# Feed-forward gate and up in seven block products, with their result kept in float32

## The chip, the cores and the metric

One NeuronCore of a Trainium2 chip runs the whole program. The time is device microseconds (us) from the first to the last instruction of one execution. The kernel before takes 2728.88 us, the median of three runs (2725.41 to 2729.14).

## What is computed

A decoder trunk of two layers on 512 tokens of width 1024, in float32. Each layer is three residual steps, each followed by a layer norm:

```python
def swiglu(x, w_gate, w_up, w_down):
    return (jax.nn.silu(x @ w_gate) * (x @ w_up)) @ w_down

for l in range(DEPTH):                                   # DEPTH = 2
    x = layer_norm(ALPHA * x + 0.5 * swiglu(x, ffn1_gate[l], ffn1_up[l], ffn1_down[l]), ...)
    x = layer_norm(ALPHA * x + token_mixing(x, w_in[l], ...), ...)
    x = layer_norm(ALPHA * x + 0.5 * swiglu(x, ffn2_gate[l], ffn2_up[l], ffn2_down[l]), ...)
```

The hidden width of the feed-forward is 2816, 22 tiles of 128 features, so there are four feed-forward passes with 22 feature tiles each. `token_mixing` is a pair of attention branches (a selected/compressed/window one and a dilated one), a spatial gating unit, three merge gates and an output product.

## The kernel before, in words

**Precision.** TensorE multiplies in float32r. Every operand is held as two float32r parts, high and low, and a product is three matmuls: high by high, high by low, low by high (`mm3`, lines 367 to 369).

**Weights.** All weights are packed into blocks of [128, 1024] in the order of their use (`PLAN`). SyncE brings one after another into `raw` (3 buffers); `split_w` makes the high part on ScalarE (line 322) and the low part on VectorE, or on GpSimd in some stretches (line 325), into `wh` and `wl` (4 buffers). `pump` and `get_w` split ahead of use, two blocks in the feed-forward.

**Feed-forward.** x stands transposed as `xh`, `xl` in the first 64 blocks (of 128 columns) of the big tile `R`. For each of 22 feature tiles f, `ffn` multiplies the gate block and the up block with x: 8 row tiles by 3 matmuls of 512 columns, for each of the two. The first two feature tiles run in two halves of 256 columns, since they start while the last token tiles are still being transposed (`x_transposed`, lines 428 to 434). `post` then takes silu on ScalarE (line 575), the product on VectorE (line 578), and the high and low parts on VectorE (lines 387, 388); all 22 results stand in `R` until `tm_gemm` has used them. `tm_gemm` (the down product) runs two passes of 512 output columns; each weight block holds two row tiles and serves 24 matmuls. The last four blocks of a pass are held so that the token tiles finish one by one and residual and norm run beside the next tile.

**Mixers.** `weave` emits two generators in turn: attention steps as they become ripe, dense products in between. Their memory comes from the 168 other blocks of `R` (`ralloc`, first fit). Where a dense step finds no room it yields WAIT, and attention steps follow one another without dense products between them.

**Order.** The program is written out in the order of emission: each engine runs its own instructions in that order, and waits are semaphores on the data they need. What stands ahead of an instruction in its engine's list therefore delays it.

## Time and profile before

| | |
|---|---|
| median of three runs | 2728.88 us |
| profiled execution, first to last instruction | 2728.7 us |
| TensorE busy | 2654.7 us (97%), 13566 matmuls |
| VectorE busy | 1256.5 us (46%) |
| ScalarE busy | 871.5 us (32%) |
| GpSimd busy | 638.0 us (23%) |

The profiled execution lies within 0.2 us of the median, and its span is all of its time: nothing lies around it. A busy share is an average over the whole program. The program has stages of two kinds: feed-forward (about 26 to 372 us, 1000 to 1720 us and from 2360 us on) and mixers (372 to 1000 us and 1720 to 2360 us), and they are to be read apart.

### The profile page before, as it was taken

What the parts mean: (1) busy time and instruction counts of PE and PEld (TensorE: products, weight loads), DVE (VectorE), ACT (ScalarE), POOL (GpSimd) and SP (SyncE); (2) the same over time, 40 slices, a digit from 0 to 9 for tenths busy, and PEclk for the clock granted to TensorE, in tenths of its full rate; (3) what the DMA queues carried; (4) which work ended last, traced back from release to release, by engine and by line L of the source; (5) the groups of instructions that cost most, each with busy time, mean ns of one, the idle gap of its engine ahead of it and who ended that gap; (6) DMA issues with size and microseconds to landing.
All of it is one profiled execution on the core that took longest, in us unless ns stands there. A gap on an engine that the chain in (4) does not pass through costs nothing. (4 is left out here: it accounts for less than half of the span.)

```text
span 2728.7 us, 34447 instructions
## 1 busy us (share of the span) xinstructions
PE 2654.7 (97%) x13566; PEld 2256.6 (83%) x13566; DVE 1256.5 (46%) x2501; ACT 871.5 (32%) x1562; POOL 638.0 (23%) x563
## 2 busy tenths in 40 slices
PE   9999999999999999999999999999999999999998
PEld 8888889977778888888888888899777788888887
DVE  4333265667442463432443333656674424633334
ACT  3222134445642222221222222345455322222211
POOL 1000015554644510000010000246455454100000
PEclk9999999999999999999999999999999999999999
DMA  4223333111212333333233232222112134322332
GB/s 165 93 95 123 100 99 100 60 47 40 78 41 91 116 119 98 94 118 103 72 103 99 93 121 95 101 92 71 36 52 65 43 99 135 106 95 96 108 101 77
DMA packets 71170, 248.16 MB, mean 91 GB/s; under 512 B 8016, under 2 KB 10096, under 8 KB 71008
## 3 DMA queue, kind: packets, MB, share of 16 engines
q1 hardware_dynamic: 68832, 238.25, 26.8%
q0 software_dynamic: 2176, 7.71, 0.9%
q8 instruction: 106, 1.74, 0.3%
q14 instruction: 56, 0.46, 0.1%
HBM read 239.64 MB, written 6.29 MB: 90 GB/s over the span
## 5 line engine op out<-in xcount | busy, mean ns | idle before, releaser
L368 PE MATMUL P<-R,wh 128*128 128x512 f32 (+1 forms) x2144 | 810.3, 378 | 7.1 <-DVE R L434 7.1
L367 PE MATMUL P<-R,wh 128*128 128x512 f32 (+1 forms) x2144 | 811.0, 378 | 1.0 <-ACT R L431 1.0
L369 PE MATMUL P<-R,wl 128*128 128x512 f32 (+1 forms) x2144 | 809.0, 377 | 0.0
L322 ACT CAST wh<-raw 128x1024 fp32r<-128x1024 f32 (+3 forms) x445 | 449.3, 1015 | 861.5 <-PE P L368 371.6
L367 PE MATMUL P<-wh,R 128*128 128x512 f32 (+3 forms) x1600 | 582.8, 364 | 2.0 <-ACT R L431 2.0
L368 PE MATMUL P<-wl,R 128*128 128x512 f32 (+3 forms) x1600 | 572.7, 358 | 4.2 <-POOL wl L325 2.1
L369 PE MATMUL P<-wh,R 128*128 128x512 f32 (+3 forms) x1600 | 572.9, 358 | 2.3 <-DVE R L434 2.1
L325 DVE TENSOR_TENSOR wl<-raw,wh 128x1024 fp32r<-128x1024 f32 (+1 forms) x289 | 349.0, 1234 | 397.6 <-ACT wh L322 397.4
L325 POOL TENSOR_TENSOR wl<-raw,wh 128x1024 fp32r<-128x1024 f32 (+5 forms) x157 | 352.6, 2253 | 755.0 <-ACT wh L322 754.2
L368 PEld LDWEIGHTS P<-R,wh 128*128 128x128 f32 x2144 | 405.4, 189 | 82.7 <-DVE R L434 9.1
L367 PEld LDWEIGHTS P<-R,wh 128*128 128x128 f32 x2144 | 405.2, 189 | 75.8 <-ACT R L431 1.9
L369 PEld LDWEIGHTS P<-R,wl 128*128 128x128 f32 x2144 | 405.4, 189 | 74.1
L368 PEld LDWEIGHTS P<-wl,R 128*128 128x128 f32 x1600 | 304.1, 190 | 43.9 <-POOL wl L325 3.2
L369 PEld LDWEIGHTS P<-wh,R 128*128 128x128 f32 x1600 | 303.5, 190 | 44.1 <-DVE R L434 3.2
L367 PEld LDWEIGHTS P<-wh,R 128*128 128x128 f32 x1600 | 304.1, 190 | 40.4 <-ACT R L431 2.2
L578 DVE TENSOR_TENSOR Fa<-Fa,P 128x512 f32<-128x512 f32 x88 | 60.5, 688 | 541.6 <-PE P L369 538.8
L471 POOL DMA_DIRECT2D Fa<-in_ln_g x6 | 3.5, 584 | 772.5 <-DVE Fa L578 563.5
L575 ACT ACTIVATE Fa<-P 128x512 f32<-128x512 f32 x88 | 52.6, 598 | 366.6 <-PE P L369 366.6
L1428 POOL TENSOR_SCALAR Fa<-Fa,ac,ga 128x128 f32<-128x128 f32 (+3 forms) x128 | 78.1, 620 | 67.4 <-DVE ac L1424 56.2
L387 DVE CAST R<-Fa 128x512 fp32r<-128x512 f32 (+2 forms) x130 | 77.9, 599 | 33.8 <-POOL Fa L1158 26.7
L1456 DVE TENSOR_TENSOR R<-P,R 128x256 fp32r<-128x256 f32 (+2 forms) x96 | 54.5, 595 | 66.5 <-ACT R L1443 66.3
L644 ACT CAST R<-P 128x256 fp32r<-128x256 f32 (+3 forms) x176 | 49.9, 322 | 103.2 <-PE P L641 102.8
(155 smaller groups left out, 2165.4 us busy)
## 6 DMA issues: line engine op xcount, KB each, us to landing
raw<-in_wts SPq DMA_DIRECT2D x400, 512.0 KB, 3.5
raw<-in_wts SPq DMA_DIRECT2D x16, 480.0 KB, 3.4
x_sp<-Fa SPq DMA_DIRECT2D x8, 512.0 KB, 5.1
Fa<-x_sp SPq DMA_DIRECT2D x8, 512.0 KB, 4.9
Fa<-in_ln_g POOLq DMA_DIRECT2D x6, 512.0 KB, 4.2
Fa<-in_ln_b POOLq DMA_DIRECT2D x6, 512.0 KB, 4.4
raw<-in_wts SPq DMA_DIRECT2D x8, 320.0 KB, 2.8
Fa<-in_x SPq DMA_DIRECT2D x4, 512.0 KB, 6.3
```

The lines of the kernel that those rows point to most:

```text
L322: nc.scalar.copy(h, r)
L325: (nc.gpsimd if self.pool_lo or n == 1 else nc.vector).tensor_tensor(lo, r, hf, op=OP.subtract)
L367: mm(out, lh, rh, start=start, stop=False)
L368: mm(out, lh, rl, start=False, stop=False)
L369: mm(out, ll, rh, start=False, stop=stop)
L387: self.nc.vector.tensor_copy(hi, src)
L471: self.nc.gpsimd.dma_start(v[:, k * D:(k + 1) * D], row.to_broadcast([128, D]))
L575: nc.scalar.activation(s, self.P[bg], AF.Silu)
L578: nc.vector.tensor_tensor(h, s, self.P[bu], op=OP.mult)
L644: self.nc.scalar.copy(hi, src[ps, ks])
L1428: t.nc.gpsimd.tensor_scalar(e, e, rd[:, br:br + 1], t.ga[:, s["i"], c:c + 1], op0=OP.mult, op1=OP.mult)
L1456: self.t.nc.vector.tensor_tensor(lo, src, h, op=OP.subtract)
```

## The change

- The weight blocks of feature tiles 2 to 21 are packed as quarters: [gate rows 0-511 | up rows 0-511] and [up rows 512-1023 | gate rows 512-1023]. Seen as a 2 by 2 matrix of blocks (gate and up by the two halves of the inner width), times x as a 2 by 2 matrix (halves of the inner width by halves of the tokens), the eight block products become seven, on sums and differences of blocks. Each product is 4 row tiles by 3 matmuls of 256 columns.
- Four sums of weight blocks for each feature tile are made on GpSimd (`quad`); each of the seven left operands is then split by itself, 512 columns at a time. Eight half buffers are handed out as they come free, and the split runs up to eight products ahead (`LOOK`).
- Four sums of x blocks are made once for each pass (`x_sums`), from a float32 copy of x transposed.
- The results of the products are put together by copies on ScalarE and additions on VectorE as they leave PSUM; the second half of the last product is a GpSimd instruction.
- The product of silu(gate) and up stays in float32 (`H`); the down product makes its high and low parts as it goes, twice, once for each pass, in ten rotating buffers (`make`).
- `H` and the upper 80 of the 232 blocks of `R` are one memory, `H` in the feed-forward, `Rb` in the mixers. The mixers' allocator may not cross the seam at block 152, and the merged results stay below it.
- All 22 feature tiles were of the old kind; tiles 0 and 1 still are (`PLAIN`).

```diff
         for f in range(NF):
-            plan.append(("kcol", f"ffn{w}_gate", l, f * 128, 1024))
-            plan.append(("kcol", f"ffn{w}_up", l, f * 128, 1024))
+            for part in range(2):
+                if f < PLAIN:
+                    plan.append(("kcol", f"ffn{w}_" + ("gate", "up")[part], l, f * 128, 1024))
+                else:
+                    plan.append(("quad", f"ffn{w}", l, (f, part), 1024))
...
-RB, FB = 232, 44
+RB, R0, FB = 232, 152, 44
+HB = RB - R0
 EB, EA = 30, 24
 XB = NT * KT
-RAW, WB = 3, 4
+RAW, WB, LOOK = 3, 4, 8
...
-    def ralloc(self, n):
-        while (a := self.ra.alloc(n)) is None:
+    def ralloc(self, n, up=False):
+        while (a := (self.ra.alloc(n, R0, RB) if up else None) or self.ra.alloc(n)) is None:
...
-        (nc.gpsimd if self.pool_lo or n == 1 else nc.vector).tensor_tensor(lo, r, hf, op=OP.subtract)
+        (nc.gpsimd if kind == "full" and (self.pool_lo or j == 1) else nc.vector).tensor_tensor(lo, r, hf, op=OP.subtract)
+        if kind == "full":
+            self.raw_done[n] = True
+        else:
+            if q in self.sums:
+                self.fa.free(self.sums.pop(q)[0], 4)
+            self.raw_done[n] |= q == S1
+            self.raw_done[n + 1] |= q == A22
...
+    def quad(self, n, q):
+        a11, a21 = (self.raw[:, n % RAW, c:c + 512] for c in (0, 512))
+        a22, a12 = (self.raw[:, (n + 1) % RAW, c:c + 512] for c in (0, 512))
+        def add(k, x, y, op):
+            a, v = self.fbuf(4)
+            self.nc.gpsimd.tensor_tensor(v, x, y, op=op)
+            self.sums[k] = (a, v)
+            return v
+        if q == A11:
+            s1 = add(S1, a21, a22, OP.add)
+            add(S2, s1, a11, OP.subtract)
+        elif q == S1:
+            add(S3, a11, a21, OP.subtract)
+        elif q == A12:
+            add(S4, a12, self.sums[S2][1], OP.subtract)
+        return {A11: a11, A12: a12, A22: a22}[q] if q in (A11, A12, A22) else self.sums[q][1]
...
+    def dma_w(self, upto=len(PLAN)):
+        while self.n_dma < upto and (self.n_dma < RAW or self.raw_done[self.n_dma - RAW]):
...
-        while (self.n_split < len(PLAN) and self.n_split < self.n_got + look
-               and (self.n_split < WB or self.done_w[self.n_split - WB])):
+        while self.n_split < min(len(JOBS), self.n_got + look) and self.w_room(self.n_split) is not None:
...
+    def new_h(self):
+        assert not any(self.ra.used[R0:])
+        self.ra.used[R0:] = [True] * HB
+        self.H = self.pool.tile([128, HB * 128], F32, name="H", tag="hr", bufs=1)
+    def new_rb(self):
+        self.Rb = self.pool.tile([128, HB * 128], F32R, name="Rb", tag="hr", bufs=1)
...
+            if ffn:
+                nc.scalar.copy(xt[:, ks, ts], src)
...
+        if ffn and i >= 2:
+            self.x_sums(i - 2)
+    def x_sums(self, j):
+        nc = self.nc
+        xt = self.H[:, :4096].rearrange("p (a k t) -> p a k t", a=2, k=4)
+        b11, b21 = (xt[:, a, :, j * 128:(j + 1) * 128] for a in range(2))
+        b12, b22 = (xt[:, a, :, j * 128 + 256:(j + 1) * 128 + 256] for a in range(2))
+        t = [self.H[:, 4096 + (j * 4 + n) * 512:4096 + (j * 4 + n + 1) * 512].rearrange("p (k t) -> p k t", k=4)
+             for n in range(4)]
+        nc.vector.tensor_tensor(t[0], b12, b11, op=OP.subtract)
+        nc.gpsimd.tensor_tensor(t[2], b22, b12, op=OP.subtract)
+        nc.vector.tensor_tensor(t[1], b22, t[0], op=OP.subtract)
+        nc.gpsimd.tensor_tensor(t[3], b21, t[1], op=OP.subtract)
+        for n in range(4):
+            hi, hif, lo = (q[:, :, j * 128:(j + 1) * 128] for q in self.xt_views(n))
+            nc.scalar.copy(hi, t[n])
+            nc.vector.tensor_tensor(lo, t[n], hif, op=OP.subtract)
...
-            ha, h = self.fbuf(4)
-            nc.vector.tensor_tensor(h, s, self.P[bu], op=OP.mult)
+            nc.vector.tensor_tensor(H(f), s, self.P[bu], op=OP.mult)
             self.unbank(bu)
             self.fa.free(sa, 4)
-            r = 0 if f == NF - 1 else self.ra.alloc(8)
-            self.hilo_sb(self.rv(r, 4), self.rvf(r, 4), self.rv(r + 4, 4), h)
-            self.fa.free(ha, 4)
-            hh.append(r)
...
-        for f in range(2, NF):
-            b = [self.bank(), self.bank()]
-            for q in range(2):
-                w = self.get_w("kcol")
-                self.fm_proj(b[q], w)
-                self.put_w(w)
-            post(f, *b)
+        x_of = lambda c, k0: tuple(q[:, k0:k0 + 4, c:c + 256] for q in (self.xh, self.xl))
+        t_of = lambda n: self.xt_views(n)[::2]
+        right = {A11: x_of(0, 0), A12: x_of(0, 4), S4: x_of(256, 4), S1: t_of(0), S2: t_of(1), S3: t_of(2), A22: t_of(3)}
+        def product(st, q, b, more=False):
+            self.n_got = max(self.n_got, st["j"] + q + 1)
+            self.pump(0)
+            _, wh, wl = w = (st["j"] + q, *self.w_views(st["j"] + q)[::2])
+            rh, rl = right[q]
+            for k in range(4):
+                ks = slice(k * 128, k * 128 + 128)
+                self.mm3(self.P[b][:, :256], wh[:, ks], wl[:, ks], rh[:, k], rl[:, k],
+                         k == 0 and not more, k == 3, more)
+            self.put_w(w)
+            self.pump(LOOK)
+        def end(st):
+            f, b = st["f"], st["beta"]
+            product(st, A22, b, True)
+            nc.vector.tensor_tensor(H(f, slice(0, 256)), st["g"][:, :256], self.P[b][:, :256], op=OP.mult)
+            self.unbank(b)
+            nc.gpsimd.tensor_tensor(H(f, slice(256, 512)), st["g"][:, 256:], st["p"], op=OP.mult)
+            self.fa.free(st["ga"], 4)
+            self.fa.free(st["pa"], 2)
+        prev = None
+        for f in range(PLAIN, NF):
+            if f == HB // 4:
+                more.append(self.fbuf((NF - f) * 4))
+            st = {"f": f, "j": self.n_got}
+            st["ga"], st["g"] = self.fbuf(4)
+            st["pa"], st["p"] = self.fbuf(2)
+            g1, g2, p = st["g"][:, :256], st["g"][:, 256:], st["p"]
+            beta, gamma, alpha = st["beta"], _, _ = [self.bank() for _ in range(3)]
+            P = [self.P[b][:, :256] for b in (beta, gamma, alpha)]
+            product(st, A11, beta)
+            nc.scalar.copy(g1, P[0])
+            product(st, S1, gamma)
+            nc.scalar.copy(p, P[1])
+            product(st, A12, alpha)
+            nc.vector.tensor_tensor(g1, P[2], g1, op=OP.add)
+            self.unbank(alpha)
+            product(st, S2, beta, True)
+            nc.scalar.copy(g2, P[0])
+            if prev:
+                end(prev)
+            product(st, S4, gamma, True)
+            nc.vector.tensor_tensor(g2, P[1], g2, op=OP.add)
+            self.unbank(gamma)
+            nc.scalar.activation(st["g"], st["g"], AF.Silu)
+            product(st, S3, beta, True)
+            nc.vector.tensor_tensor(p, P[0], p, op=OP.add)
+            prev = st
             if l + j == 0 and f == 4:
                 self.load_consts()
+        end(prev)
+        self.ra.free(self.xt_at, 64)
+        base = self.ra.alloc(80)
+        made, used, hs = [0], [0], NT * 2
+        def make(n):
+            a = base + n % 10 * 8
+            v = H(n % NF)
+            self.nc.scalar.copy(self.rv(a, 4), v)
+            self.nc.vector.tensor_tensor(self.rv(a + 4, 4), v, self.rvf(a, 4), op=OP.subtract)
         def lhs(k):
-            r = hh[k]
-            return self.rv(r, 4), self.rv(r + 4, 4)
-        self.tm_gemm(lhs, NF, l, j, last)
-        for r in hh[:-1]:
-            self.ra.free(r, 8)
-    # ---- mixers ----
+            n = k if used[0] < NF else NF + k
+            while made[0] < min(max(n + 5, used[0] + 8), used[0] + 10, 2 * NF):
+                make(made[0])
+                made[0] += 1
+            assert made[0] > n >= used[0]
+            a = base + n % 10 * 8
+            return self.rv(a, 4), self.rv(a + 4, 4)
+        def done(k):
+            used[0] += 1
+        self.tm_gemm(lhs, NF, l, j, last, done)
+        self.ra.free(base, 80)
+        self.fa.free(more[0][0], (NF - HB // 4) * 4)
...
-            r = yield from self.ralloc(8)
+            while (r := self.ra.alloc(8, 64, R0)) is None:
+                yield WAIT
             self.mg.append(r)
```

**What the change moves in the lists of the engines.** Each list is in the order in which its engine runs it; "x2" is two of the same in a row.

**VectorE and GpSimd, one feature tile of gate and up.** Before, on VectorE (line 578 is the product with up, 387 and 388 its two parts, 325 the low parts of two weight blocks):

```order
L578 TENSOR_TENSOR Fa<-Fa,P_74 128x512
L387 CAST R<-Fa 128x512
L388 TENSOR_TENSOR R<-Fa,R 128x512
L325 TENSOR_TENSOR wl<-raw,wh 128x1024 x2
L578 TENSOR_TENSOR Fa<-Fa,P_76 128x512
```

GpSimd has no arithmetic in this stage before. Now VectorE has this for a feature tile (line 389 makes the low part of a left operand, from `raw` or from a sum in `Fa`; 784, 791 and 795 add what left PSUM; 763 is the first half of the last product):

```order
L389 TENSOR_TENSOR wl<-raw,wh 128x512
L389 TENSOR_TENSOR wl<-Fa,wh 128x512
L389 TENSOR_TENSOR wl<-raw,wh 128x512
L784 TENSOR_TENSOR Fa<-P_74,Fa 128x256
L389 TENSOR_TENSOR wl<-Fa,wh 128x512
L389 TENSOR_TENSOR wl<-raw,wh 128x512
L763 TENSOR_TENSOR H<-Fa,P_78 128x256
L389 TENSOR_TENSOR wl<-Fa,wh 128x512
L791 TENSOR_TENSOR Fa<-P_73,Fa 128x256
L389 TENSOR_TENSOR wl<-Fa,wh 128x512
L795 TENSOR_TENSOR Fa<-P_75,Fa 128x256
```

Seven splits of 512 columns stand where two of 1024 stood, and four instructions of 256 columns that read PSUM stand between them. GpSimd now has, for the same feature tile, the four sums (line 407) and half of the last product (line 765):

```order
L407 TENSOR_TENSOR Fa<-raw 128x512
L407 TENSOR_TENSOR Fa<-Fa,raw 128x512
L407 TENSOR_TENSOR Fa<-raw 128x512
L407 TENSOR_TENSOR Fa<-raw,Fa 128x512
L765 TENSOR_TENSOR H<-Fa 128x256
```

GpSimd's part of a feature tile is new, and each of its five instructions reads SBUF twice.

**VectorE and ScalarE, from gate and up to the down product of the first pass.** Before, on VectorE:

```order
L578 TENSOR_TENSOR Fa<-Fa,P_72 128x512
L387 CAST R<-Fa 128x512
L388 TENSOR_TENSOR R<-Fa,R 128x512
L325 TENSOR_TENSOR wl<-raw,wh 128x1024 x11
L477 SCALAR_TENSOR_TENSOR Fa<-P_77,Fa 128x512
```

The parts of the last feature tile were made by `post`; from there on only weight blocks were split (325), until the first residual (477). Now, on VectorE (809 makes the low part of a row tile of the down product):

```order
L791 TENSOR_TENSOR Fa<-P_76,Fa 128x256
L389 TENSOR_TENSOR wl<-raw,wh 128x1024
L795 TENSOR_TENSOR Fa<-P_78,Fa 128x256
L389 TENSOR_TENSOR wl<-raw,wh 128x1024
L763 TENSOR_TENSOR Fa<-Fa,P_78 128x256
L809 TENSOR_TENSOR R<-H,R 128x512 x10
L389 TENSOR_TENSOR wl<-raw,wh 128x1024
L809 TENSOR_TENSOR R<-H,R 128x512 x2
```

and on ScalarE (386 splits weights, 793 is silu, 808 makes the high part of a row tile):

```order
L787 COPY Fa<-P_78 128x256
L386 CAST wh<-raw 128x1024
L793 ACTIVATE Fa<-Fa 128x512
L386 CAST wh<-raw 128x1024 x2
L808 CAST R<-H 128x512 x10
L386 CAST wh<-raw 128x1024
```

The first ten row tiles of the down product are now split after the last product of gate and up, and behind the fourth split of a whole weight block.

**TensorE in the mixers, first layer, after the transposes that end the second projection of the dilated head 1.** Before, the projection of the next head followed (320 columns, lines 367 to 369):

```order
L641 MATMUL P_74<-ident,Fa 128x128 x2
L367 MATMUL P_75<-wh,R 128x320
L368 MATMUL P_75<-wl,R 128x320
L369 MATMUL P_75<-wh,R 128x320
L367 MATMUL P_75<-wh,R 128x320
L368 MATMUL P_75<-wl,R 128x320
```

Now an attention step follows there (lines 460 to 462 are `mm3`, 1504 and 1505 scores of the third group, 1547 transposes of weights):

```order
L845 MATMUL P_72<-ident,Fa 128x128 x2
L460 MATMUL P_77<-Rb 128x128
L461 MATMUL P_77<-Rb 128x128
L462 MATMUL P_77<-Rb 128x128
L460 MATMUL P_75<-Rb 128x128
L461 MATMUL P_75<-Rb 128x128
L462 MATMUL P_75<-Rb 128x128
L1504 MATMUL P_74<-R 128x128
L1505 MATMUL P_74<-R 128x128
L1547 MATMUL P_78<-ident,Fa 128x128 x2
L1547 MATMUL P_72<-ident,Fa 128x128 x4
L1547 MATMUL P_77<-ident,Fa 128x128 x4
```

The projection of that head comes later, because 18 blocks are free at this point but no run of 12 on one side of the seam; it is the same number of products in another order.

## Rows read from the trace of the kernel before

**Rows 1.** The page, parts 1 and 2: busy us, granted TensorE clock.

```profile
PE 2654.7 (97%) x13566; PEld 2256.6 (83%) x13566; DVE 1256.5 (46%) x2501; ACT 871.5 (32%) x1562; POOL 638.0 (23%) x563
...
PEclk9999999999999999999999999999999999999999
```

**Rows 2.** Busy time by stage: stretch, length, each engine, PEclk, DMA share, GB/s.

```profile
26.00:372.00 346.00, 346.00 (x1574) 288.38 (x1573) 131.25 (x166) 80.87 (x92) 4.34 (x6) 1.00 0.32 101
372.00:1000.00 628.00, 600.62 (x3391) 519.17 (x3390) 341.72 (x882) 263.01 (x582) 300.64 (x265) 0.98 0.25 79
...
1720.00:2360.00 640.00, 611.39 (x3447) 528.08 (x3446) 352.16 (x903) 267.00 (x588) 302.86 (x266) 0.98 0.24 79
```

**Rows 3.** Timeline of TensorE, gate and up at 512 columns: start, us, engine, line.

```profile
60.06 0.39 PE L369 MATMUL P<-R,wl 128*128 128x512 f32 x1
...
63.91 0.39 PE L368 MATMUL P<-R,wh 128*128 128x512 f32 x1
```

**Rows 4.** Timeline of VectorE, one feature tile of gate and up.

```profile
243.47 0.69 DVE L578 TENSOR_TENSOR Fa<-Fa,P 128x512 f32<-128x512 f32 x1 [6.73 <-PE P L369]
...
244.66 0.69 DVE L388 TENSOR_TENSOR R<-Fa,R 128x512 fp32r<-128x512 f32 x1
245.27 2.36 DVE L325 TENSOR_TENSOR wl<-raw,wh 128x1024 fp32r<-128x1024 f32 x2
254.35 0.69 DVE L578 TENSOR_TENSOR Fa<-Fa,P 128x512 f32<-128x512 f32 x1 [6.73 <-PE P L369]
```

**Rows 5.** Timeline of TensorE and its weight load, products of 256 columns.

```profile
13.10 0.28 PE L367 MATMUL P<-R,wh 128*128 128x256 f32 x1
...
16.10 0.28 PE L368 MATMUL P<-R,wh 128*128 128x256 f32 x1
16.10 0.19 PEld L369 LDWEIGHTS P<-R,wl 128*128 128x128 f32 x1
```

**Rows 6.** Groups by line and shape: busy us, mean ns | idle before.

```profile
L322 ACT CAST wh<-raw 128x1024 fp32r<-128x1024 f32 x399 | 417.3, 1049 | 848.3 <-PE P L368 371.6 <-PE P L369 348.1 <-issue 46.5
L575 ACT ACTIVATE Fa<-P 128x512 f32<-128x512 f32 x88 | 52.6, 598 | 366.6 <-PE P L369 366.6
...
L644 ACT CAST R<-P 128x256 fp32r<-128x256 f32 x64 | 22.2, 374 | 59.4 <-PE P L641 59.4
...
L648 DVE TENSOR_TENSOR R<-P,R 128x256 fp32r<-128x256 f32 x64 | 25.1, 416 | 14.4 <-ACT R L644 14.4
...
L1158 POOL TENSOR_TENSOR Fa<-Fa 128x512 f32<-128x512 f32 x32 | 41.3, 1289 | 28.5 <-DVE Fa L1154 28.2
```

**Rows 7.** Timelines of VectorE and GpSimd at the end of the first pass.

```profile
359.41 1.27 DVE L485 SCALAR_TENSOR_TENSOR Fa<-Fa,ac 128x1024 f32<-128x1024 f32 x1
...
372.36 6.29 POOL L325 TENSOR_TENSOR wl<-raw,wh 128x840 fp32r<-128x840 f32 x3 [147.40 <-ACT wh L322]
379.33 2.25 POOL L325 TENSOR_TENSOR wl<-raw,wh 128x960 fp32r<-128x960 f32 x1 [0.69 <-ACT wh L322]
...
375.35 2.47 DVE L434 TENSOR_TENSOR R<-P,R 128x512 fp32r<-128x512 f32 x4
...
379.50 3.17 DVE L485 SCALAR_TENSOR_TENSOR Fa<-Fa,ac 128x1024 f32<-128x1024 f32 x1
```

**Rows 8.** Timelines of TensorE and VectorE where the second pass starts.

```profile
998.71 0.39 PE L368 MATMUL P<-R,wh 128*128 128x256 f32 x1 [1.84 <-DVE R L434]
...
1006.56 1.28 DVE L434 TENSOR_TENSOR R<-P,R 128x512 fp32r<-128x512 f32 x2
1012.33 1.29 DVE L434 TENSOR_TENSOR R<-P,R 128x512 fp32r<-128x512 f32 x2 [4.49 <-ACT R L431]
```

**Rows 9.** Busy time in one stretch of a mixer without dense work.

```profile
540.00:560.00 20.00, 17.93 (x126) 16.25 (x125) 10.45 (x35) 8.60 (x22) 9.90 (x9) 0.91 0.17 54
```

**Rows 10.** The page, part 6: weight DMAs, KB each, us to landing.

```profile
raw<-in_wts SPq DMA_DIRECT2D x400, 512.0 KB, 3.5
```

More of the change, by code (lines that the diff above doesn't have):

```diff
@@ L33 @@
 GATES_AHEAD = 2
+PLAIN = 2
 def weight_plan():
@@ L94, with weight_jobs @@
 PLAN = weight_plan()
+def weight_jobs():
+    jobs = []
+    for n, p in enumerate(PLAN):
+        if p[0] != "quad":
+            jobs.append(("full", n, 0))
+        elif p[3][1] == 0:
+            jobs += [("quad", n, q) for q in range(7)]
+    return jobs
+JOBS = weight_jobs()
+A11, S1, A12, S2, A22, S4, S3 = range(7)
 def pack_weights(inp):
@@ L102, in pack_weights @@
             o[:].reshape(128, KT, 128)[...] = inp[name][l][:, a:a + 128].reshape(KT, 128, 128).transpose(1, 0, 2)
+        elif kind == "quad":
+            f, part = a
+            for h, nm in enumerate(("gate", "up") if part == 0 else ("up", "gate")):
+                src = inp[f"{name}_{nm}"][l][part * 512:part * 512 + 512, f * 128:f * 128 + 128]
+                o[:, h * 512:h * 512 + 512].reshape(128, 4, 128)[...] = src.reshape(4, 128, 128).transpose(1, 0, 2)
         elif kind == "rows":
@@ L192, in alloc @@
         for a in list(range(at, hi)) + list(range(lo, at)):
+            if self.seam and a < self.seam < a + n:
+                continue
             if a + n <= hi and not any(self.used[a:a + n]):
@@ L241, in __init__ @@
         self.n_dma = self.n_split = self.n_got = 0
-        self.done_w = [False] * len(PLAN)
+        self.raw_done = [False] * len(PLAN)
+        self.w_free = deque(range(2 * WB))
+        self.w_at = {}
+        self.sums = {}
         self.pool_lo = False
@@ L360, in put_w, with mm3 @@
     def put_w(self, w, look=0):
-        self.done_w[w[0]] = True
+        at, n = self.w_at[w[0]]
+        self.w_free.append(at)
+        if JOBS[w[0]][0] == "full":
+            self.w_free.append(at + 1)
         if look and not self.weaving:
             self.pump(look)
-    def mm3(self, out, lh, ll, rh, rl, start, stop):
+    def mm3(self, out, lh, ll, rh, rl, start, stop, more=False):
         mm = self.nc.tensor.matmul
-        mm(out, lh, rh, start=start, stop=False)
-        mm(out, lh, rl, start=False, stop=False)
-        mm(out, ll, rh, start=False, stop=stop)
+        mm(out, lh, rh, start=start, stop=False, skip_group_check=more)
+        mm(out, lh, rl, start=False, stop=False, skip_group_check=more)
+        mm(out, ll, rh, start=False, stop=stop, skip_group_check=more)
     def defer(self, f, wait=LATE):
@@ L508, in tm_gemm @@
                 self.put_w(w)
+                done(n * 2)
+                done(n * 2 + 1)
             if h == 0:
@@ L570, in ffn, with H @@
         nc = self.nc
-        hh = []
+        more = []
+        def H(f, c=slice(0, 512)):
+            at = f - HB // 4
+            q, o = (self.H, f * 512) if at < 0 else (more[0][1], at * 512)
+            return q[:, o + c.start:o + c.stop]
         def post(f, bg, bu):
@@ L592, in ffn @@
             self.ensure_x(2 * cb + 1)
-            for f in range(2):
+            for f in range(PLAIN):
                 if cb == 0:
```

103 lines of the change are left out of this document (71 added, 32 removed).

## The prediction

> **What bounds the kernel now.** I read the page first: TensorE is busy for 97% of the span at full granted clock, no other engine for half of it [rows 1]. Then the stages, since an average hides them. In the gate and up and down products TensorE never pauses: 346 of 346 us, with VectorE at 131 and GpSimd at 4 us [rows 2]. The mixers leave it idle for 27 and 29 us. So the feed-forward goes as fast as TensorE can take its instructions, and a change there is worth what it takes off TensorE's list, until another engine becomes late. Then the pace of that list: at 512 columns one matmul starts every 3.85 us / 17 starts = 0.2265 us [rows 3]. VectorE confirms it from outside: its feature tiles are 10.88 us apart, which is 48 matmuls, and it waits 6.73 us of each for TensorE [rows 4].
>
> **The seven products.** This rests on the pace at 256 columns, which the kernel before also shows, where a pass starts: 3.00 us / 25 starts = 0.120 us [rows 5]. That is more than half of 0.2265: about 13 ns of each matmul do not shrink with its columns. A feature tile was 2 x 8 x 3 = 48 matmuls, 10.88 us. It becomes 7 x 4 x 3 = 84, 10.08 us. The saving is 0.80 us, not the eighth (1.36 us) that the arithmetic promises. Four passes have 20 such tiles: **-64 us**. The weight load beside each matmul takes 0.19 us, longer than the pace [rows 5], and yet the pace is 0.12: it overlaps two neighbours and does not set it.
>
> The Trainium skill (TensorE: Matmul & The Clock Gate, Part 3, "The mechanism") says that a weight load overlaps running matmuls only if it goes to other rows of the array. Every load here fills all of it, so load and matmul would add up: a tile would go from 48 x (0.19 + 0.2265) = 20 to 84 x (0.19 + 0.12) = 26 us, and the change would cost 6 us in each. The pace of rows 5 excludes that, so it has no share among the rivals.
>
> **What is added beside TensorE, per feature tile.** ScalarE: seven splits at half of 1.05 us, three copies at 0.37, one silu at 0.60 [rows 6]: 5.4 of 10.08 us. VectorE: seven low parts of 512 columns at half of 1.23 us, so 0.61 [rows 4], and four instructions of 256 columns that read PSUM, at 0.42 [rows 6]: 6.0 us. GpSimd: 2.25 us for 960 columns [rows 7] is 1.20 for 512 and 0.60 for 256; four sums and a half product are 5.4 us (the 1.29 of rows 6 includes waits). Each fits alone. The DMA brings the same two blocks of 512 KB as before, 3.5 us each [rows 10]; the buffer of the first is free after the third sum, and 3.5 us plus the next three sums, each with a VectorE split between (3 x 1.8), is 8.9 us, also under 10.08.
>
> But VectorE and GpSimd hold each other up. A VectorE instruction with two SBUF inputs that takes 1.27 us alone took 3.17 when it was issued 0.17 us after a GpSimd one of 2.25, and four with one input in PSUM kept 0.62 each beside GpSimd [rows 7]. So the seven low parts (4.3 us) and GpSimd's 5.4 us exclude each other: 9.7 of 10.08 us. That fits barely, if VectorE's PSUM instructions fall beside GpSimd's. If every GpSimd instruction stopped VectorE in full, VectorE would need 6.0 + 5.4 = 11.4 us for a tile, +1.3 us x 80 = +106 us. The bounds are 0 and +106. I take **+4 us**, near the lower one, because VectorE is idle for some 4 us of a tile, waiting for TensorE's next product, and a GpSimd instruction that runs there costs nothing; and because the left operands are split seven products ahead, so that 7 x 1.44 us (12 matmuls each) of lateness reach TensorE only by a detour: silu on ScalarE waits for an addition on VectorE, and ScalarE's copies must be done before the same PSUM bank is added to, which allows two products, 2.9 us.
>
> **From gate and up to down.** Before, the ten first row tiles stood split. Now the first of them comes, on VectorE, after the fourth whole weight block, whose buffer the very last product frees, and after the last half product. From the end of that product: ScalarE's split 1.05 [rows 6], VectorE's low part 1.23, the half product 0.42, the low part of the first row tile 0.69 [rows 4, 6] = 3.4 us, in which TensorE can do two matmuls of high parts (0.45). So 2.9 us, four times: **+12 us**. Bounds: +3 (only 0.42 + 0.69 late, if that weight block takes an earlier buffer) to +24 (VectorE arrives 3 us late besides).
>
> **Where a pass starts.** TensorE already waited 1.84 us for a low part of x there [rows 8]. Between the low parts of token tiles 2 and 3, VectorE now has two sums and four low parts (6 x 0.69 = 4.1 us), with two GpSimd sums that can stop it (2 x 1.2). Free from 1007.8 us on, it would be done at 1014.3, where it took up tile 3 at 1012.33 [rows 8]. 2.0 us late, some of it before TensorE asks: 1.5 us, four times, **+6 us** (0 to +16).
>
> **Down.** 44 row tiles are split in each pass, where 22 were in gate and up. For the two tiles that go with one weight block VectorE needs 1.23 + 2 x 0.69 = 2.6 and ScalarE 1.05 + 2 x 0.53 = 2.1 us [rows 4, 6], beside 24 matmuls x 0.2265 = 5.44 us, ten tiles ahead. I cost it at nothing. Without that cover it would be 1.4 us for a block.
>
> **Mixers.** The seam changes no product, only the order: in each mixer a run of some 15 attention steps without dense work appears after head 1, and one of the same length after head 3 goes. Such a stretch had 2.07 us of idle TensorE and a lower granted clock, 0.91 [rows 9]. I take **+2 us** for both mixers (-4 to +8).
>
> **Sum.** -64 + 4 + 12 + 6 + 2 = -40, against the profiled execution's 2728.7 us, all of it span and within 0.2 us of the median: **2689 us**.
>
> **Rivals.**
> 1. *Slower: VectorE and GpSimd set the pace.* The lock serialises them and, once VectorE is late, a bubble adds to it: after the addition that silu waits for, VectorE's next split waits for ScalarE's silu and split (0.60 + 0.53 us). The other terms give back 20 of the 64 us, so it decides from 44 / 80 = 0.55 us more for a tile, 10.63 us. At 11.0 us, between 10.08 and 11.4, the sum is +74 - 44 = +30: 2759 us. For it speaks that 9.7 of 10.08 us are excluded already; against it that GpSimd's instructions come in one bunch that can run well ahead, and VectorE's idle time. 17%.
> The Trainium skill (SBUF — State Buffer, "Who interferes with whom") has it as a rule: a VectorE instruction with two SBUF inputs and a GpSimd one that reads SBUF take turns, the second to issue waiting in full, and one with at most one SBUF input is free of it. By that rule, the trace agrees (3.17 for 1.27, and 0.62 unchanged), this rival has its mechanism; the rule does not say who idles meanwhile.
> 2. *Half of that*: 10.4 us for a tile, +26 - 44 = -18: 2711 us. 17%.
> 3. *No change*: 10.6 us, +42 - 44 = -2: 2727 us. 8%.
> 4. *The edges are hidden and the lock costs nothing*: -64 + 4 = -60: 2669 us. The low ends of the bounds allow it; against it, TensorE already waits at a pass's start. 10%.
> That the seven products don't pay on TensorE needs another pace at 256 columns: 10.88 / 84 = 0.130 us would do it, and rows 5 show 0.120 in an unbroken run, so I give it no share of its own.
>
> **How the numbers follow.** The forecast has 48%, with an own range of 2676 to 2702 (its three small terms at their middle bounds). Faster by over 0.2% (5.5 us, about what a measurement of this kernel can tell from no change) are the forecast, rivals 2 and 4: 75%. Within it is rival 3: 8%. Slower: 17%. The range that leaves out half of rival 4 below and most of rival 1 above is 2667 to 2738 us.
>
> **What would show it.** TensorE's 256-column matmuls in gate and up at 0.120 us, and feature tiles 10.1 us apart on VectorE; if they are 10.6 or more apart, with TensorE waiting for `wl` low parts of line 389 or for ScalarE's copies, rivals 1 to 3 hold. GpSimd's sums at 1.2 us, those of VectorE's low parts that meet them at up to 1.8. A wait of about 3 us of TensorE for line 809 at the start of each down product, and one of 1 to 3 us for line 540 where a pass starts. Idle time of TensorE in the mixers still near 28 us each. The forecast is wrong if waits inside gate and up add up to more than 20 us.

## The result, and the profile after

The changed kernel takes **2766.35 us** (median of 4 runs, 2761.78 to 2768.66), where the kernel before took 2729.01 in the same job: a ratio of 1.0135, 95% interval [1.012, 1.0149]. It is 37 us slower. The forecast was 2689 us, 40 faster, and the range ended at 2738.

The page of the changed kernel, part 1, in the columns of [rows 1]:

```profile
PE 2630.4 (95%) x16446; PEld 2369.3 (86%) x16446; DVE 1769.6 (64%) x3187; ACT 1233.1 (45%) x2442; POOL 1234.2 (45%) x981
```

TensorE's idle time, span less busy time, went from 2728.7 - 2654.7 = 74 us [rows 1] to 2762.5 - 2630.4 = 132 us: 58 us more. The mean granted clock fell from 0.991 to 0.977. With two levels, 1.2 and 2.4 GHz, that is about (1 - 0.991) x 2 x 2728.7 = 49 us at half clock before and 127 us after: 78 more. Work done at half clock takes nearly twice its time (at the edge below a 256-column matmul starts every 0.214 us there, in place of 0.120), so up to 39 us are lost. TensorE's busy time agrees: it fell by 24 us and not by 64, so 40 are lost in it. So -64 us of matmuls, +58 of waits and up to +39 behind them give up to +33; the profiled spans differ by 33.8. The question is which waits.

First what came true. TensorE in the middle of gate and up of the second pass, timeline as in [rows 5]:

```profile
1149.94 0.28 PE L462 MATMUL P<-R,wl 128*128 128x256 f32 x1
...
1151.74 0.28 PE L462 MATMUL P<-R,wl 128*128 128x256 f32 x1
```

Fifteen starts in 1.80 us are 0.120 us each, as forecast from [rows 5]. And VectorE's last addition of two feature tiles there, which answers to [rows 4]:

```profile
1154.27 0.41 DVE L795 TENSOR_TENSOR Fa<-P,Fa 128x256 f32<-128x256 f32 x1
...
1164.35 0.41 DVE L795 TENSOR_TENSOR Fa<-P,Fa 128x256 f32<-128x256 f32 x1
```

A tile takes 10.08 us, where it took 10.88. The matmuls that the seven products save are saved, and VectorE and GpSimd do not set the pace there.

The list of TensorE's waits, changed kernel: engine, tile and line waiting, what released it, us in total, times, longest.

```profile
PE P L460 <- DVE Fa L795: 17.6, 4, 4.4
PE P L460 <- ACT R L537: 13.9, 7, 3.2
PE P L1574 <- DVE R L1561: 12.3, 4, 4.3
PE P L1547 <- POOL Fa L1531: 11.9, 9, 2.1
...
PE P L460 <- ACT Fa L780: 9.1, 11, 1.8
...
PE P L460 <- ACT R L808: 5.8, 4, 1.4
...
PE P L461 <- DVE R L540: 4.4, 7, 0.8
PE P L462 <- DVE R L540: 4.1, 2, 2.1
```

The two ends of a pass lead it: the edge to down (L795, L808: 23.4 us) and the start (L537, ScalarE's casts of x). L1574 and L1547 are in the mixers, L780 is the first copy of a tile. The same waits at the start of a pass in the kernel before:

```profile
PE P L368 <- DVE R L434: 7.1, 8, 1.8
...
PE P L367 <- ACT R L431: 2.9, 5, 2.0
...
PE P L369 <- DVE R L434: 2.1, 1, 2.1
```

The waits for VectorE's low parts of x (line 434, now 540) did not grow: 9.2 us before, 8.5 now. Those for ScalarE's casts (line 431, now 537) went from 2.9 to 13.9. So what the start of a pass adds comes from ScalarE, where the float32 copies and the casts of the x sums now stand ahead of the next token tile's casts: in the second pass the copies of tile 0 start at 1012.58, after 2.83 us of waiting for VectorE, three weight casts follow, and the casts of tile 1 come at 1016.50.

Now the edge itself, second pass: timelines of TensorE, VectorE and ScalarE, then windows (stretch, length, busy time of each engine with its instructions, PEclk, DMA share, GB/s).

```profile
1256.50 0.58 PE L460 MATMUL P<-R,wh 128*128 128x256 f32 x1 [4.41 <-DVE Fa L795]
1256.88 0.41 PE L461 MATMUL P<-R,wh 128*128 128x256 f32 x1
...
1259.02 0.41 PE L462 MATMUL P<-R,wl 128*128 128x256 f32 x1
1260.87 0.79 PE L460 MATMUL P<-wh,R 128*128 128x512 f32 x1 [1.44 <-ACT R L808]
...
1262.55 0.79 PE L462 MATMUL P<-wh,R 128*128 128x512 f32 x1 [0.45 <-DVE R L809]
```

```profile
1254.89 1.23 DVE L389 TENSOR_TENSOR wl<-raw,wh 128x1024 fp32r<-128x1024 f32 x1 [1.63 <-ACT wh L386]
1256.03 0.42 DVE L795 TENSOR_TENSOR Fa<-P,Fa 128x256 f32<-128x256 f32 x1
```

```profile
1253.29 0.63 ACT L793 ACTIVATE Fa<-Fa 128x512 f32<-128x512 f32 x1 [1.63 <-DVE Fa L791]
1253.83 1.03 ACT L386 CAST wh<-raw 128x1024 fp32r<-128x1024 f32 x1
```

```profile
1255.00:1260.00 5.00, 2.93 (x12) 2.63 (x12) 1.45 (x2) 0.75 (x1) 1.79 (x3) 0.50 0.61 197
1260.00:1265.00 5.00, 3.67 (x8) 2.47 (x9) 4.67 (x8) 5.00 (x11) 0.00 (x0) 0.50 0.79 251
1265.00:1270.00 5.00, 5.00 (x18) 3.95 (x17) 2.91 (x5) 0.50 (x1) 0.00 (x0) 0.72 0.07 25
```

The last A22 adds into the bank that S3 has just written, and may start only when the addition L795 has read S3's sum out of it. In every other tile A22 runs four products later, behind A11, S1, A12 and S2 of the next tile; the last tile has no next one. L795 stands in VectorE's queue behind the split of a weight block of down (1254.89), that one waits for its cast (1253.83), and the cast for silu (1253.29). TensorE stands still for 4.41 us, then 1.44 and 0.45: 6.3 us. From 1255 to 1265 it is granted half of its clock, and for some 2.8 of the next 5 us; up to (2.93 + 3.67 + 2.8) / 2 = 4.7 us of its work are lost there. 11 us, four times, would be 44 us.

Where the first pass is in its third tile of the new kind, GpSimd's timeline and two windows:

```profile
76.46 1.68 POOL L509 CAST masks<-Fa 128x1792 bf16<-128x1792 f32 x1 [6.54 <-DMA Fa<-in_consts]
```

```profile
75.00:80.00 5.00, 2.41 (x21) 2.21 (x19) 0.00 (x0) 0.60 (x2) 3.46 (x3) 1.00 0.07 28
80.00:85.00 5.00, 4.66 (x28) 4.66 (x28) 4.95 (x5) 2.77 (x7) 5.00 (x4) 0.66 0.31 93
```

The constants' cast waits 6.54 us for its DMA on GpSimd, and the sums stand behind it.

### The profile page after: what moved, and what is told of

Read it like the earlier page. It is cut to its first block, busy times and chain, and to the rows that moved or that the text cites. A ratio compares the mean times of both kernels' runs of the same rounds, so it can differ in the third digit from the quotient of the medians.

```text
span 2762.5 us, 43188 instructions
## 1 busy us (share of the span) xinstructions
PE 2630.4 (95%) x16446; PEld 2369.3 (86%) x16446; DVE 1769.6 (64%) x3187; ACT 1233.1 (45%) x2442; POOL 1234.2 (45%) x981
## 5 line engine op out<-in xcount | busy, mean ns | idle before, releaser
L460 PE MATMUL P<-R,wh 128*128 128x256 f32 (+1 forms) x2976 | 905.5, 304 | 44.3 <-DVE Fa L795 17.6
L461 PE MATMUL P<-R,wh 128*128 128x256 f32 (+1 forms) x2976 | 901.5, 303 | 4.4 <-DVE R L540 4.4
L462 PE MATMUL P<-R,wl 128*128 128x256 f32 (+1 forms) x2976 | 900.7, 303 | 0.8 <-POOL wl L389 0.8
L386 ACT CAST wh<-raw 128x1024 fp32r<-128x1024 f32 (+4 forms) x525 | 429.6, 824 | 546.1 <-PE P L462 261.6
L389 POOL TENSOR_TENSOR wl<-raw,wh 128x1024 fp32r<-128x1024 f32 (+4 forms) x159 | 352.2, 2222 | 704.6 <-ACT wh L386 701.1
L460 PEld LDWEIGHTS P<-R,wh 128*128 128x128 f32 x2976 | 576.4, 194 | 69.2 <-DVE Fa L795 18.4
L389 DVE TENSOR_TENSOR wl<-raw,wh 128x512 fp32r<-128x512 f32 (+2 forms) x367 | 402.0, 1098 | 353.3 <-ACT wh L386 352.9
L461 PEld LDWEIGHTS P<-R,wh 128*128 128x128 f32 x2976 | 576.8, 194 | 24.5 <-DVE R L540 6.1
L462 PEld LDWEIGHTS P<-R,wl 128*128 128x128 f32 x2976 | 576.8, 194 | 20.5 <-POOL wl L389 1.0
L389 DVE TENSOR_TENSOR wl<-Fa,wh 128x512 fp32r<-128x512 f32 x320 | 361.7, 1131 | 117.3 <-ACT wh L386 116.4
L407 POOL TENSOR_TENSOR Fa<-raw 128x512 f32<-128x512 f32 x160 | 227.7, 1423 | 199.8 <-DMA raw<-in_wts 189.0
L386 ACT CAST wh<-Fa 128x512 fp32r<-128x512 f32 x320 | 197.1, 617 | 158.3 <-PE P L461 85.0
```

The costliest lines, as they stand in the source:

```text
L386: nc.scalar.copy(h, r)
L389: (nc.gpsimd if kind == "full" and (self.pool_lo or j == 1) else nc.vector).tensor_tensor(lo, r, hf, op=OP.subtract)
L407: self.nc.gpsimd.tensor_tensor(v, x, y, op=op)
L460: mm(out, lh, rh, start=start, stop=False, skip_group_check=more)
L461: mm(out, lh, rl, start=False, stop=False, skip_group_check=more)
L462: mm(out, ll, rh, start=False, stop=stop, skip_group_check=more)
```

## The experiments

All ran in 5 rounds against the kernel before (2728.8 to 2729.6 us in each job). "After" is the changed kernel, 2766.35 us. "Counted matmul by matmul" means that the n-th matmul of one trace is set against the n-th of another, so that a gain is seen where it arises.

**The edge rewritten.** In the last tile each copy or addition goes ahead of the next weight split, the A22 of the tile before moves between S3 and the last A22, so that the addition has a product to cover it, and six row tiles of down are split early.

```diff
-            product(st, S3, beta, True)
+            product(st, S3, beta, True, tail)
             nc.vector.tensor_tensor(p, P[0], p, op=OP.add)
+            if tail:
+                early(2)
+                end(prev, True)
+                self.pump(LOOK)
...
-        end(prev)
+        end(prev, True)
```

> The changed kernel with another order in the last feature tile of each pass: the last product but one tile's (A22 of tile 20) goes behind S3 of tile 21, what leaves PSUM is put ahead of the next weight split on its engine, six row tiles of the down product are split during the last products, and the last two products are followed by no weight split. Theory 1 (the gain of the seven products is lost at the edges of a pass; the end of gate and up costs 6.3 us of waits and 10 to 14 us at 1.2 GHz in each of four passes): 30 to 45 us less than the changed kernel, 2722 to 2736 us, with no granted clock below 1 there. Theory 2 (VectorE and GpSimd exclude each other, the feed-forward as a whole is late, and a wait taken away here comes back behind it): less than 10 us.

Measured: 2723.3 us, ratio 0.9983 [0.9974, 0.9992]: **43 us less** than after, and this edit alone ends the loss. The windows over the same edge:

```profile
1235.00:1240.00 5.00, 5.00 (x43) 4.97 (x42) 4.10 (x9) 3.82 (x7) 0.74 (x1) 1.00 0.32 105
1240.00:1245.00 5.00, 5.00 (x23) 4.13 (x22) 5.00 (x7) 3.39 (x6) 1.11 (x2) 1.00 0.65 146
```

TensorE is busy throughout, at full clock. Counted matmul by matmul, the four edges give 10.1, 11.3, 9.8 and 10.4 us, 41.7 in all. What the edge costs is shown; which of the three parts of the edit gives how much is not. Outside the edges the two traces drift apart by up to 5 us either way in each mixer stage, which this edit does not touch: differences of 7 us, as below, are to be held against that.

**The edge filled.** Of the 43 us only 23.4 are in the list of waits. Throwaway matmuls keep TensorE at work over them.

```diff
+        fill(36)
         end(prev)
+        fill(14)
```

> The changed kernel with throwaway matmuls at the edge of every pass, and nothing else: 36 of 256 columns (4.3 us by the pace of 0.120 us) ahead of the last tile's A22, where TensorE waited 4.4 us for the addition, and 14 (1.7 us) behind it, where it waited 1.4 us for the first split of down. They keep TensorE at work over the waits and speed nothing else up. The edge cost 43 us (the run with the edge rewritten), of which the waits themselves are 23.4 us (17.6 and 5.8 by the list of waits). Theory (the rest is the half clock that the waits bring on behind them): the waits stay as busy time, the half clock at 250, 1260, 1625 and 2625 us goes, about 20 us less, so 2746 (2740 to 2752). Rival (the clock falls there for another reason, or the rest of the 43 us was the rewritten order and not the clock): 2766, or a little above.

Measured: 2752.35 us, ratio 1.0088 [1.0075, 1.0102], **14 us less** than after, just beyond the theory's upper end of 2752. Windows of the edge and what was left there in the list of waits:

```profile
1251.00:1256.00 5.00, 4.91 (x41) 4.68 (x39) 2.06 (x3) 1.74 (x4) 1.80 (x3) 1.00 0.68 184
1256.00:1261.00 5.00, 4.06 (x18) 3.02 (x17) 5.00 (x9) 4.67 (x9) 0.00 (x0) 1.00 0.77 299
```

```profile
PE P L462 <- DVE R L818: 3.8, 4, 0.9
```

The clock stays at 1.00: doing useless work made the kernel faster. The theory's size was too large, in part because the fillers (200 x 0.12 = 24 us) and a wait of 3.8 us left over took 28 us where the waits had taken 25 (23.4 and four times 0.45). So the half clock behind the waits is at least 14 of the 43 us, and by this sum some 17.

**The pass start reordered.** The float32 copies of x of the first two token tiles (ScalarE) go behind the first products, and the splits of the first x sums (ScalarE and VectorE) go behind the parts of the last token tile.

```diff
-            if ffn:
...
+        def keep():
+            for b, src, ks, ts in jobs:
                 nc.scalar.copy(xt[:, ks, ts], src)
-            self.unbank(b)
+                self.unbank(b)
+        if ffn and i < 2:
+            self.xt_later.append(keep)
```

> The changed kernel with another order where a pass starts: the float32 copies of x of token tiles 0 and 1 leave PSUM only after the first products are listed, and the splits of the x sums of tiles 0 and 2 go behind the parts of tile 3. Theory 1 (ScalarE's and VectorE's lists at the start hold TensorE up, 5.1 + 1.2 us of waits in the second pass and 6.8 us at 1.2 GHz): 6 to 16 us less, 2750 to 2760 us. Theory 2 (exclusion): the same work in the same stretch, 0 to 3 us.

Measured: 2759.36 us, ratio 1.0115 [1.0101, 1.0129], 7 us less than after (some 5 either way, by the two intervals). The list of waits:

```profile
PE P L461 <- ACT Fa L799: 18.3, 14, 2.1
...
PE P L462 <- DVE R L541: 6.9, 7, 1.8
```

The waits for ScalarE's casts of x are gone (13.9 us before, 1.0 now), those for VectorE's low parts are not (line 541 is what 540 was; 11.0 us with the 4.1 of another line), and the wait for a tile's first copy (L799 here, L780 in after) doubled from 9.1 to 18.3 us: more than half of the gain was passed on to the next wait.

**The constants later**, behind the first gate and up.

```diff
-            if l + j == 0 and f == 4:
-                self.load_consts()
...
+        if l + j == 0:
+            self.load_consts()
```

> The changed kernel with the five GpSimd DMAs of constants and the copy of the masks moved from feature tile 4 of the first pass to its end. Theory 1 (the sums stood behind the copy, which waited 6.54 us for its DMA, and the one interval of 17.7 us between feature tiles, where 10 is usual, is that wait): 7 to 10 us less, 2756 to 2760 us, all in that interval. Theory 2 (exclusion): GpSimd's instructions are only moved, 0 to 2 us.

Measured: 2759.18 us, ratio 1.0112 [1.0098, 1.0126], 7 us less than after (again some 5 either way). From 75 to 85 us TensorE is busy for 10 us of 10, where it was for 7.07 and at a clock of 0.66 in the second 5:

```profile
75.00:80.00 5.00, 5.00 (x44) 5.00 (x43) 5.00 (x7) 2.99 (x7) 3.03 (x3) 1.00 0.30 96
80.00:85.00 5.00, 5.00 (x44) 5.00 (x44) 3.50 (x6) 2.51 (x5) 4.03 (x3) 1.00 0.34 114
```

Counted matmul by matmul, 4 us are gained between 60 and 95 us; the rest of the 7 is no more than the drift.

**The sums left out**, a run that did not answer its question.

```diff
-            a, v = self.fbuf(4)
-            self.nc.gpsimd.tensor_tensor(v, x, y, op=op)
-            self.sums[k] = (a, v)
-            return v
+            self.sums[k] = (None, x)
+            return x
```

> The changed kernel without the four weight sums of each feature tile: one block of raw weights is split in place of each sum, so the result is another one; all products, splits and copies stay. GpSimd keeps one instruction of 256 columns for a tile. Theory 1 (edges; the feature tiles in the middle already take 10.0 us): 8 to 20 us less, from the first tiles of each pass and from the constants, nothing at the end of gate and up. Theory 2 (exclusion of VectorE and GpSimd is what costs): 35 us or more less, below 2730 us.

Measured: 3119.05 us, ratio 1.1434 [1.1418, 1.1449]. Neither theory has that. From ScalarE's list of waits:

```profile
ACT wh L386 <- DMA raw<-in_wts: 488.4, 121, 7.0
```

With x in place of the sum, S2 and S3 are cast from a raw buffer that is handed to the next DMA as soon as S1 is split (S4 from the other one, handed on after A22), so the casts wait for that DMA. The run measured raw buffers handed on too early and nothing of GpSimd; the question is put again below.

**The allocator's rules alone, on the kernel before.** Eight products stay.

```diff
-            A[name] = yield from self.ralloc(n)
+            A[name] = yield from self.ralloc(n, name == "q")
...
-            o = yield from self.ralloc(8)
+            o = yield from self.ralloc(8, True)
```

> The kernel before with one part of the change alone: only the allocator's rules (the seam in the shared memory, upper blocks wanted for q and for the outputs, lower blocks for one kind of result); eight products stay. In the changed kernel the two mixer stages took 12.5 and 6.8 us longer than before, and these rules alone put the dense work and the mixers' steps into the changed kernel's order. Theory (the order of dense work and mixer steps costs that): about +15 us on 2729, so 2744 (2738 to 2750), with some 5 us more idle TensorE in each mixer stage. Rival (the order is neutral; the mixer stages grew by what stands around them, the clock after the passes and the starts of the next ones): 2729, within 5 us.

Measured: 2750.28 us, ratio 1.0075 [1.0062, 1.0088], **21 us more** than the kernel before. TensorE's list in the mixers is then that of the changed kernel. TensorE is idle for 10 us more (84 against 74) and busy for 9 us more with the same matmuls; counted matmul by matmul, 11 us are lost in the first mixer stage, 5 in the second and 1.5 at the start of the pass behind each.

**The old order, on the changed kernel**: all four results of the B projections are asked for in upper blocks.

```diff
-            B[name] = yield from self.ralloc(n)
+            B[name] = yield from self.ralloc(n, True)
```

> The changed kernel, where all four results of the B mixer's projections are asked for in upper blocks first, which gives the dense work back the order against the mixers' steps that it had before the change. Theory (that order costs): about -15 us on 2766, so 2751 (2745 to 2757). Rival (neutral): 2766, within 5 us.

Measured: 2744.94 us, ratio 1.0053 [1.004, 1.0066], **21 us less** than after. TensorE's list in the mixers is that of the kernel before again. Busy time from the first residual addition of the first down product to that of the first mixer's merge, for four kernels: before, changed, before with the allocator's rules, changed with the old order.

```profile
310.00:969.00 659.00, 633.46 (x3529) 546.33 (x3528) 343.43 (x879) 267.00 (x584) 294.19 (x262) 0.98 0.25 80
```

```profile
315.00:986.00 671.00, 639.80 (x3527) 550.96 (x3526) 359.07 (x894) 274.58 (x600) 297.25 (x263) 0.98 0.23 79
```

```profile
311.00:980.00 669.00, 637.51 (x3527) 549.61 (x3526) 349.23 (x878) 266.65 (x584) 297.00 (x263) 0.98 0.24 79
```

```profile
317.00:973.00 656.00, 631.05 (x3526) 542.90 (x3525) 352.70 (x895) 274.78 (x599) 294.60 (x262) 0.99 0.24 81
```

The same matmuls take 659, 671, 669 and 656 us: the stage follows the order and not the feed-forward around it. Both runs went further than 15 us, in opposite directions, and the rival (neutral) falls.

**The four edits together.**

> The changed kernel with four edits: the edge between gate/up and down (by itself -43), the pass start (-7), the constants moved behind the first gate/up (-7), and the mixers' order as in the run beside it. If the four are independent and the mixers' order costs 15: 2766 - 43 - 7 - 7 - 15 = 2694 (2686 to 2702). If the mixers' order is neutral: 2709. If the start's and the constants' gains were only slack that other waits take up: 2715 to 2723.

Measured: **2693.39 us**, ratio 0.9868 [0.9854, 0.9883]. The four edits give 73 us, by themselves 43 + 7 + 7 + 21 = 78: nearly independent. This kernel is 4 us from the forecast, which is chance: what is left in it are other terms than the forecast's, as the next runs show.

**Every copy and addition ahead of the next weight split**, not only in the last tile. The edit against the kernel with the four edits:

```diff
-            product(st, A11, beta, hold=tail)
+            product(st, A11, beta, hold=True)
             nc.scalar.copy(g1, P[0])
-            if tail:
-                self.pump(LOOK)
+            self.pump(LOOK)
```

> The kernel with the four edits, and in every feature tile of the seven products each bank's copy or addition is issued ahead of the next weight block's cast instead of behind it (in the four edits only the last tile had that). Theory (the waits of TensorE for the first copy of a tile, 12 to 18 us in sum in the runs so far, come from the casts that stand ahead of it on ScalarE, and bring half clock behind them): 15 us less than the kernel with the four edits, near 2680. Rival (the casts come later then, and the next product waits for its weights instead): as much as the kernel with the four edits, or more.

Measured: 2685.49 us, ratio 0.9836 [0.9824, 0.9849], 8 us less than the four edits. The waits for the first copy fell by 9 us, from the first of these lines (four edits) to the second, and what waits for weight splits rose from 3.3 to 6.0:

```profile
PE P L461 <- ACT Fa L814: 15.1, 12, 1.8
...
PE P L463 <- DVE wl L390: 3.3, 4, 0.8
```

```profile
PE P L461 <- ACT Fa L814: 6.3, 8, 1.1
PE P L463 <- DVE wl L390: 6.0, 8, 0.8
```

Half of the theory's 15 us, then; the waits for weight splits, the rival's, took back 2.7 us.

**The sums left out again**, the raw buffers' lives unchanged, on that kernel. What is multiplied is then not gate and up; the number of casts, splits and matmuls stays.

```diff
+        big = self.Raf[:, 0:512]
+        return {A11: a11, S1: a21, A12: a12, S2: a12, S4: big, S3: big, A22: a22}[q]
```

> The fastest kernel so far (2685) without the four sums on GpSimd: S1 and S2 are cast from a21 and a12 of the raw blocks, S3 and S4 from a fixed piece of memory that is always there, so that the raw buffers come free as before; every cast, split and matmul stays. The product's values are then not gate and up. Theory (VectorE's and GpSimd's mutual exclusion is off the path: tiles go by TensorE's pace, 84 matmuls of 0.120 us): 2685, within 4 us, with tiles of 10.0 us still. Rival (the exclusion still costs what the prediction priced, 4 us, or more at the starts of the passes): 2670 to 2681, with shorter tiles or earlier first tiles.

Measured: 2665.14 us, ratio 0.9766 [0.9753, 0.9779], **20 us less**, and 5 below the rival's lower end too. My theory falls: GpSimd's sums were on the path. But the steady tiles are no shorter than in after (line 825 is what 795 was):

```profile
1131.60 0.42 DVE L825 TENSOR_TENSOR Fa<-P,Fa 128x256 f32<-128x256 f32 x1
...
1141.68 0.42 DVE L825 TENSOR_TENSOR Fa<-P,Fa 128x256 f32<-128x256 f32 x1
```

The time comes from where a pass starts: counted matmul by matmul, the four starts give 3.9, 4.6, 6.2 and 5.2 us, and the tiles behind them nothing. VectorE there, second pass, with the sums (the kernel of 2685 us) and then without:

```profile
1004.03 2.48 DVE L581 TENSOR_TENSOR R<-H,R 128x512 fp32r<-128x512 f32 x4
...
1008.75 5.80 DVE L581 TENSOR_TENSOR R<-H,R 128x512 fp32r<-128x512 f32 x4
1014.47 1.77 DVE L390 TENSOR_TENSOR wl<-raw,wh 128x512 fp32r<-128x512 f32 x1
...
1018.46 0.68 DVE L390 TENSOR_TENSOR wl<-Fa,wh 128x512 fp32r<-128x512 f32 x1
```

```profile
1004.76 3.59 DVE L567 TENSOR_TENSOR R<-H,R 128x512 fp32r<-128x512 f32 x4
1008.27 2.49 DVE L390 TENSOR_TENSOR wl<-raw,wh 128x512 fp32r<-128x512 f32 x4
```

From the second four x splits to the fourth weight split VectorE takes 10.4 us with the sums (1008.75 to 1019.14) and 6.0 without, 4.4 us more, near the 4.6 that this start gives. VectorE has no pause there that could take it up: with the sums it is busy for 19.8 of the 20 us from 1004 on. The Trainium skill (SBUF — State Buffer, "Who interferes with whom") says that a VectorE instruction with two SBUF inputs and a GpSimd one that reads SBUF exclude each other; these rows agree, 1.77 us beside sums and 0.62 without. Leaving the sums out also takes away the waits of the casts for their sums; how much of the 20 us is that is not separated.

**Three sums of a pass's first tile earlier.**

```diff
                     self.ensure_x(2 + f)
+                    if f == 0:
+                        self.presum()
```

> The fastest full kernel so far (2685) with three of the first tile's four sums (S1, S2, S3) issued on GpSimd earlier in each pass, behind the first pair of x sums, where GpSimd waits 4.2 us for ScalarE (1002.3 to 1006.4 in pass 2), instead of behind the second pair, where they met VectorE's splits: there four splits of the x sums took 5.80 us and each weight split 1.77, against 3.59 and 0.68 in the run without sums, and the kernel without sums was 20 us faster. Theory (what costs is that the exclusion meets VectorE while TensorE waits for it; moved to where VectorE has 2 us of room in 4, part of it goes): 2 to 3 us less in each pass, 2675 to 2679. Rival (VectorE and GpSimd only share what both need, and the x splits and low parts that come first grow as much as the later ones shrink): 2685, within 4 us.

Measured: **2679.04 us**, ratio 0.9814 [0.9801, 0.9827], 6 us less, the upper end of the theory (1 to 2.5 us in each pass, counted matmul by matmul, where 2 to 3 were expected). VectorE at the same place:

```profile
1001.18 5.37 DVE L592 TENSOR_TENSOR R<-H,R 128x512 fp32r<-128x512 f32 x4
...
1012.50 0.68 DVE L390 TENSOR_TENSOR wl<-raw,wh 128x512 fp32r<-128x512 f32 x1
```

The rival's mechanism is there as well: the first four x splits, which the sums now meet, take 5.37 us where they took 2.48, and the weight splits are back at 0.68. The exclusion was moved to a place with room for a part of it. It is the fastest full kernel here, 1.9% faster than before.

## Why the prediction was wrong, point by point

| term | predicted | shown | by |
|---|---|---|---|
| seven products | -64 | -64 | the second run without sums, where the other terms are gone: 2665 against 2729 |
| edge to down | +12 | +43 | the edge rewritten |
| pass start | +6, VectorE's | +7, ScalarE's | its reorder and the list of waits |
| VectorE and GpSimd | +4 | +20 | the second run without sums |
| mixers | +2 | +21 | both runs on the order |
| constants | none | +7 (4 at the place itself) | constants later |
| copies behind splits | none | +8 | copies ahead of splits |

The shown terms add up to +42, and +37 was measured: the four edits' gains overlap by 5. That is no check of its own, since the rows are the steps from the changed kernel to the run without sums; the two rows of +7 may each be off by some 5. The first row rests on a kernel whose idle time is that of before: busy for 2593.3 us of 2665.3, 72 idle against 74, so that what is left between them is matmuls.

```profile
PE 2593.3 (97%) x16446; PEld 2343.5 (88%) x16446; DVE 1558.5 (58%) x3189; ACT 1233.9 (46%) x2442; POOL 748.1 (28%) x659
```

- **The step that failed** is the edge: "From the end of that product: ScalarE's split 1.05 [rows 6]", with +12 us and bounds of +3 to +24. It counted from the end of A22, and took for granted that A22 follows S3 at once. What it says about the time behind A22 is near: the first matmul that needs a low part of down starts 3.3 us behind A22's end, 3.4 were forecast, and 1.44 + 0.45 = 1.9 us of it are waits, for 2.9. It missed the 4.41 us ahead of A22. A bank's readers are covered by the products that run until it is written again (two for the copies, as the prediction says, and four for S3's addition), and for the last tile these four are not there. The call `end(prev)` behind the loop shows it. The waits alone, 25 us, come to the upper bound of +24; the half clock behind them, which had no term, did the rest.
- **A wait was priced as its length.** [Rows 9] had it: 17.93 us of 20 busy, so 2.07 idle, at a clock of 0.91, which is up to another 1.8 us lost. At the edge the filler shows at least 14 us on top of 23.4.
- **The mixers** were mis-sized: +2 with bounds of -4 to +8, shown 21. The changed order was seen and its price taken from one stretch.
- **The lock**, +4, was right for the steady tiles, which came out at TensorE's own 10.08, so rival 1 is wrong (it needed 10.63), though its 2759 us is near the result. It was too small where a pass starts, for there VectorE has no idle time to hide a GpSimd instruction in: I had 2.4 us of stops in the pass start's term and had left out the first tiles' own sums and weight splits. GpSimd was also under-priced: its five instructions of a steady tile are busy for 7.25 us (from 1149.45 us on) where 5.4 were forecast, and no sum took less than 1.25 us, so the 1.29 of [rows 6], which the prediction put down to waits, was near the price.
- **The constants** have no term: their call stood in that loop before the change too, but there nothing that TensorE waits for stood behind it on GpSimd (GpSimd did 4 us in 346, [rows 2]). Every instruction of an engine that gets onto the path must be looked at again, the old ones too.
- **The pass start** was right in size by luck. The prediction has VectorE late at line 540, but those waits did not grow (9.2 to 8.5 us); TensorE waited for ScalarE's casts (2.9 to 13.9 us), behind copies for which the prediction had no time at the start of a pass.
- Seven products and down: as predicted. Behind its first three matmuls down shows no wait of TensorE.

Open: the 21 us of the mixers are tied to the order, half as waits and half as longer busy time, and not to one of its waits. The rest of the 20 us of the sums, 14, was not recovered.

## What to carry to other kernels

When a pipelined loop gets a longer chain per step, price its first and its last turn by themselves: list for each engine what stands ahead of the instruction that TensorE waits for when there is no next step to cover it. Put the instructions that free a bank ahead of those that prepare the work after next, in every turn. Price a wait of TensorE at more than its length, since the work behind it may run at half clock, and don't take the right total for the right mechanism: here a rival's time was near and its cause was absent.

## What the runs showed of the hardware

That work which serves nothing saves time: 200 matmuls, 24 us of TensorE, in place of most of 25 us of waits, made the kernel 14 us faster; the granted clock stayed at 1.00 where it had been 0.50. And that the exclusion of VectorE and GpSimd can be moved (weight splits of 1.77 us back to 0.68, x splits from 2.48 to 5.37 for four), with a gain of 6 us though no work was taken away.
